# Norm sums that move the squares, in column quarters, and three smaller moves in a two-layer hybrid backbone

## Chip, cores and metric

The kernel runs on one core of a Trainium2 chip. The metric is the device time of one execution in microseconds; the time of a kernel is the median of its runs. TensorE is called PE in the profile, its weight loads PEld, VectorE DVE, ScalarE ACT, GpSimd POOL and SyncE SP; a q behind a name (SPq, ACTq) is that engine's queue of DMA issues and waits.

## The reference, cut to what matters

512 latent tokens and 256 context tokens of 1024 channels go through two layers. Layer 0 mixes by a Fourier transform beside a bidirectional state-space scan (SSD), layer 1 by differential attention of 8 heads beside a conformer convolution; each mixer and each feed-forward network (FFN) is framed by RMSNorms, and scaled and shifted by modulation vectors that come from the conditioning.

```python
def rmsnorm(x, g):
    xf = x.astype(jnp.float32)
    y = xf * lax.rsqrt(jnp.mean(xf * xf, axis=-1, keepdims=True) + NORM_EPS)
    return (y * g.astype(jnp.float32)).astype(x.dtype)
...
        m = (jax.nn.silu(c) @ mod_w[i] + mod_b[i]).reshape(-1, N_MOD, 1, D_MODEL)
        a_h = modulate(rmsnorm(h, g[0]), m[:, 0], m[:, 1])
        ...
        h = h + m[:, 2] * rmsnorm(o_h, g[1])
        f_h = swiglu(modulate(rmsnorm(h, g[2]), m[:, 3], m[:, 4]), ffn_w_gate[i], ffn_w_up[i], ffn_w_down[i])
        h = h + m[:, 5] * rmsnorm(f_h, g[3])
```

## The kernel before

Activations lie channel-major: 128 partitions by 8 channel groups (KT) by 768 tokens (T), the 512 latent tokens in front of the 256 of the context. Tokens are handled in three blocks of 256 (`BLK`, called a, b and c in the code; c is the context). Every large product runs in three passes over a split into a rounded part and its rest (`mm3`, L124; `split`, L97 on ScalarE and L98 on VectorE or GpSimd). Weights come in units of 512 KB through SyncE's queue into a few raw buffers (L108 for the mixers, L1189 for the FFNs), and a raw buffer is free for the next load when its split has read it. The program is traced in the written order; a scheduler with a cost model of the chip then sets the order on every engine. `tc.high_priority` and `tc.issue_after` push that order one way, and memory that a closed pool leaves is handed to the next one, whose first users wait for the last users of the old.

The stages, by the time of the profile: the first norm, the modulation vectors of layer 0 and the first projections (to about 130 us), the Fourier branch and the SSD groups (to 720), the end of the mixer and the FFN of layer 0 (to 1345), the attention with the conformer branch (to 1900), the FFN of layer 1 (to the end).

*Norms.* `rstd_stages` makes the reciprocal root for a block of 256 tokens. Squares come from ScalarE (`squares`, L290). PE then sums over channels: a group of 128 tokens of the squares is the stationary operand, one column of ones the moving one, 8 matmuls for each of 2 token groups (L263; f32 counts as two records each in the profile). The result has one column for each token group. ScalarE's root (L268) and a reciprocal on VectorE (L269) work on these two columns in the tile `nq`, and two matmuls with the reciprocals as stationary operand and the identity moving spread them over all partitions (L275). The `Turn` class strings these steps together with the residual additions: `r1` (squares and gates), `r2a`/`r2b` (norm of a branch's output and the addition), `q2`, `p1`, `p2` (norm of the sum, scale, shift and split into the inputs `xh`, `xl` of the next products), `last` for the end. Each 1024-channel norm of a block passes through `rstd_stages`; the norms of an attention head and of the conformer (one channel group, count 128 or 512) do too.

*Start.* `mod_sum` (L593) multiplies the two conditioning columns by raw modulation weights: two stationary columns, 512 moving ones, two matmuls for each of 8 groups, for vector 1 and then for vector 0. `mod_turn` copies the two rows out (L600) and turns them by eight narrow transposes (L603). Later vectors already use column quarters (`mod_quarters`, L196): four matmuls whose stationary operand is 32 wide, each writing another quarter of the partitions. The raw modulation weights pass through five buffers (L589).

*Between the mixer and the FFN of layer 0.* `turnc` handles the context block inside the SSD stage, in the pool `cp`; `h_c` is its residual, stored to the scratch `rd` (L1125). `res` then gets blocks a and b from the input and c from `rd` over ScalarE's queue (L1149, L1150). `pre0` turns a and b and stores all three blocks to `rd` (L1172). `hu` are the first three weight units of the FFN; `head(b)` runs them on a block as soon as it is ready.

*Attention.* For heads 0 to 6, four score blocks (`scores`, L1658 and L1662) each; between them `fills` are spread, first the next head's k, q and v, then what `extra` has for this head: `conv` (the conformer's convolution, L1544), `glu` (its gate, two weight units), `out_group` (output product of two finished heads). `conf_mean` and `conf_norm` follow a given head. Modulation vectors of layer 1 are summed on VectorE meanwhile (`mod_vec1`, L184 and L186), two weight loads for each score block of heads 0 to 3.

Of the kernel before, what the change touches and what calls it, by code (L numbers as in the profile page):

```python
# [21 lines left out]
KT = 8  # L22
# [34 lines left out]
def backbone_kernel(ctx, tc, xt, vec, dtrow, dskip, lam, w_mod, w_gate, w_up, w_down, w_in0, w_out0, w_in1, w_out1,  # L57
# [27 lines left out]
    qmask = cs[:, 640:644]  # L85
    eps = cst.tile([128, 1], F32, name="eps")
    nc.vector.memset(eps, EPS)
    newt = cst

    def vcol(off, n=1):  # L90
# [162 lines left out]
        return r  # L253

    fence = [None]

    def rstd_stages(psum1, sq, count, copy=True):
        n = sq.shape[-1]
        ps = psum1()
        kt = sq.shape[1]  # L260
        for h in range(n // 128):
            for k in range(kt):
                at = nc.tensor.matmul(ps[:, h:h + 1], sq[:, k, h * 128:h * 128 + 128], ones[:, 0:1], start=(k == 0),  # L263
                                      stop=(k == kt - 1))
        fence[0] = at.ins
        q = nrm[0].tile([128, 4], F32, tag="nq", name="nq", bufs=2)[:, 0:n // 128]
        if count == 1024:
            nc.scalar.activation(q, ps[:, 0:n // 128], AF.Sqrt, bias=eps, scale=1.0 / count)  # L268
            nc.vector.reciprocal(q, q)  # L269
        else:  # L270
            rsqrt(q, ps[:, 0:n // 128], count)
        yield None
        ps2 = psum1()
        for h in range(n // 128):
            at = nc.tensor.matmul(ps2[:, h * 128:h * 128 + 128], q[:, h:h + 1].to_broadcast([128, 128]), ident,  # L275
                                  start=True, stop=True)
        fence[0] = at.ins
        if not copy:
            yield ps2[:, 0:n]
            return  # L280
        r = nrm[0].tile([128, nrm[1]], F32, tag="nr", name="nr", bufs=512 // nrm[1])[:, 0:n]
        nc.scalar.copy(r, ps2[:, 0:n])
        yield r
# [233 lines left out]
    with ExitStack() as es:  # L517
# [71 lines left out]
            return raw, nc.sync.dma_start(out=raw, in_=w_mod[0, j, k]).ins  # L589

        def mod_sum(mps, raw, k):
            for n in range(2):
                nc.tensor.matmul(mps[n][0:2, :], silc[:, k, :], raw[:, n * 512:(n + 1) * 512],  # L593
                                 start=(k == 0), stop=(k == KT - 1))

        def mod_turn(mps, j):
            mrow = np_.tile([2, 1024], F32, tag="mrow", name="mrow", bufs=1)
            mt = psmm(2)[:, 0:16].rearrange("p (k w) -> p k w", w=2)
            for i in range(2):
                (nc.vector.tensor_copy, nc.scalar.copy)[i](mrow[:, i * 512:(i + 1) * 512], mps[i][0:2, :])  # L600
                for q in range(4):
                    b = i * 4 + q
                    turn = nc.tensor.transpose(mt[:, b, :], mrow[:, b * 128:(b + 1) * 128], ident[0:2, 0:2]).ins  # L603
            for w in range(2):
                nc.vector.tensor_tensor(out=mod[:, 0, w, j, :], in0=mt[:, :, w], in1=vcol(V_MODB + 8 * j, 8), op=ADD)
                mod_done(0, w, j)
            return turn

        mps = [psum1() for i in range(2)]
        load_x(BLK[0])  # L610
        nx = norm_x(BLK[0])
        for k in range(KT):
# [10 lines left out]
            load_x(b)  # L623
        hps = [psmm() for _ in hu]
        scaled(BLK[0])
        mps = [psum1() for i in range(2)]
        raws = [mod_raw(0, k)[0] for k in range(KT)]
        with tc.issue_after(turn):
            n1, n2 = (norm_x(b) for b in BLK[1:])
# [183 lines left out]
    with ExitStack() as es:  # L813
# [292 lines left out]
        for g in range(4):  # L1106
            if g < 3:
                xs = xbc_items(groups[g + 1])
                zs = sum([z_block(b) for b in zmap[g]], [])
                fills = merge(xs, zs)  # L1110
            else:
                state["acc"] = big.tile([128, KT, T], F32, tag="S0", name="acc")
                state["ys"] = big.tile([128, KT, T], F32R, tag="S1", name="ys")
                esx.close()
                cp = nrm[0] = pool(es, "cp", side="right")
                state["h"] = cp.tile([128, KT, 256], F32, name="h_c")
                nc.sync.dma_start(out=state["h"], in_=xt[:, :, BLK[2]])
# [27 lines left out]

    big2 = pool(ctx, "big2")
    res = big2.tile([128, KT, T], F32, tag="R", name="res")
    for b in BLK[:2]:
        nc.scalar.dma_start(out=res[:, :, b], in_=xt[:, :, b])  # L1149
    nc.scalar.dma_start(out=res[:, :, BLK[2]], in_=rd[:, :, BLK[2]])  # L1150
    xh = big2.tile([128, KT, T], F32R, tag="F0", name="xh")
    xl = big2.tile([128, KT, T], F32R, tag="F1", name="xl")

# [2 lines left out]
    def pre0(psum1, head):  # L1156
        c, a, b = BLK[2], BLK[0], BLK[1]
        t = turn0
        t.r1(a)
        t.p2(c)  # L1160
        t.r2(a, psum1)
        t.r1(b)
        head(c)
        t.q2(a)
        t.p1(a, psum1)
        t.r2(b, psum1)
        t.p2(a)
        t.q2(b)
        head(a)
        t.p2(b, psum1)  # L1170
        for blk in BLK:
            nc.scalar.dma_start(out=rd[:, :, blk], in_=res[:, :, blk])  # L1172
        head(b)
        return t.whole()
# [65 lines left out]
    def ffn(l, xh, xl, nt, pre, extra, post, spare):  # L1240
        with ExitStack() as es:
# [28 lines left out]
            todo = [(w, 2 * i + j) for i in range(NH // 2) for w in (0, 1) for j in range(2)]  # L1270
            if nu == 3:
                todo[1], todo[2] = todo[2], todo[1]
            hu = [wts.unit((w_gate, w_up)[w][l, i]) for w, i in todo[:nu]]
            hps = {wi: [bank() for _ in range(nt // 512 + (nt > 512))] for wi in todo[:nu]}

            def head(b):
# [152 lines left out]
    def post0(acc, psum1, accb):  # L1429
# [29 lines left out]
        t.p2(a)  # L1459
        fenced(c, range(3, KT))  # L1460
        t.r1(c)
        held, nrm[0] = nrm[0], cst
        t.r2a(c, psum1)
        nrm[0] = held
        t.q2(b)
        nc.scalar.dma_start(out=rd[:, :, b], in_=res[:, :, b])

# [5 lines left out]
    with ExitStack() as es:  # L1473
# [258 lines left out]
        def head1(b):  # L1732
            for u, p in list(zip(hu, hps))[3 if b.start == SEQ else 0:]:
# [21 lines left out]
        head_k(hs[0], hps[3])  # L1755
        head_v(hs[0], hps[4])

        extra = {0: [conv, lambda: glu(1)], 1: [conv, lambda: glu(2)], 2: [conv, lambda: glu(3)], 3: [conv],
                 4: [lambda: out_group((0, 1))], 5: [lambda: out_group((2, 3))]}
        late, later = [], []  # L1760
        macc = sxf[:, 4 * XN:4 * XN + 1024]

# [12 lines left out]
        for h in range(7):  # L1775
            H = hs[h]
            fills = [lambda: head_k(hs[h + 1]), lambda: head_q(hs[h + 1]), lambda: head_v(hs[h + 1])]
            fills += extra.get(h, [])
            n, done = len(fills), 0
            for qb in range(4):  # L1780
                p0 = scores(H, qb)
# [6 lines left out]
                if qb % 2 == 1:  # L1788
                    late.append(lambda H=H, qp=qb // 2: mix_v(H, qp))
                    if qb == 3:  # L1790
                        late.append(lambda H=H: sub_norm(H, LAT))
            if h == 4:
                csq = conf_mean()
            if h == 5:
                conf_norm(csq)


# [67 lines left out]
    turn2.h = Blocks({0: h_a, 256: res[:, :, b]})  # L1865

    def pre1(psum1, head):
        a, b = BLK[:2]
        turn2.r1(b)
        turn2.r2(b, psum1)  # L1870
# [142 lines left out]
```

## Time and profile before

| | |
|---|---|
| median of 3 runs | 2306.39 us (2297.15 to 2313.38) |
| the profiled execution | 2299.36 us, span 2297.6 us, mean granted clock 0.959 |
| PE busy | 2172.3 us, 95% of the span, 13742 matmul records |
| DVE, ACT, POOL busy | 1562.8, 1116.2, 758.9 us |
| read from and written to HBM | 206.51 MB and 19.63 MB |

The page gives the busy time of each engine, the chain of work that ended last, and groups of instructions by line. Other views used below: stretches (busy time of each engine between two times, with the clock that was granted to PE, the busy share of the DMA engines and GB/s; for one line alone if asked), the waits (who waited for whom, us in total, times, longest), the chain in order of time, and the instructions in order of time. A form such as "128x1 f32" is what a matmul moves, "128*32" the size of its stationary operand. Times are from the span's start.

### The profile page before, as it was taken

What the parts mean: (1) busy time and instruction counts of PE and PEld (TensorE: products, weight loads), DVE (VectorE), ACT (ScalarE), POOL (GpSimd) and SP (SyncE); (2) the same over time, 40 slices, a digit from 0 to 9 for tenths busy, and PEclk for the clock granted to TensorE, in tenths of its full rate; (3) what the DMA queues carried; (4) which work ended last, traced back from release to release, by engine and by line L of the source; (5) the groups of instructions that cost most, each with busy time, mean ns of one, the idle gap of its engine ahead of it and who ended that gap; (6) DMA issues with size and microseconds to landing.
All of it is one profiled execution on the core that took longest, in us unless ns stands there. A gap on an engine that the chain in (4) does not pass through costs nothing.

```text
span 2297.6 us, 35527 instructions
## 1 busy us (share of the span) xinstructions
PE 2172.3 (95%) x13742; PEld 1922.1 (84%) x13742; DVE 1562.8 (68%) x2551; ACT 1116.2 (49%) x2024; POOL 758.9 (33%) x703
## 2 busy tenths in 40 slices
PE   7999999898998999999999998999999888999998
PEld 3778888786787989999999997776777788999998
DVE  4722576677784566667767658767676855988985
ACT  4433586767452553333333444455555634644443
POOL 0201567676640023333334111011132110555550
PEclk9999999999999799999999979999999888999998
DMA  7344212223320533322122324555111221333321
GB/s 269 103 164 159 80 62 79 77 74 101 97 75 21 185 132 113 129 90 76 65 69 70 101 95 125 153 153 153 56 37 40 81 98 48 102 102 102 110 93 55
DMA packets 88776, 229.48 MB, mean 100 GB/s; under 512 B 8800, under 2 KB 39520, under 8 KB 88608
## 3 DMA queue, kind: packets, MB, share of 16 engines
q1 hardware_dynamic: 69584, 204.50, 27.0%
q10 hardware_dynamic: 17552, 17.61, 2.4%
q0 software_dynamic: 1472, 5.11, 0.6%
q8 instruction: 108, 1.77, 0.3%
q14 instruction: 60, 0.49, 0.1%
HBM read 206.51 MB, written 19.63 MB: 98 GB/s over the span
## 4 chain that ended last, share of the span: by engine, by line
PE 69%; DVE 13%; DMA 6%; ACT 6%; issue 3%; POOL 2%; ACTq 0%; SPq 0%; DVEq 0%; POOLq 0%
PE ps_mm L124 56%; DMA raw<-in_w_mod_dram 2%; PE ps_s L263 2%; DMA raw<-in_w_in_dram 2%; DVE w L98 1%; PE ps_s L196 1%; PE ps_s L593 1%; PE ps_mm L1544 1%; PE ps_s L911 1%; DMA mraw<-in_w_mod_dram 1%; DVE w L949 1%; PE ps_at L124 1%; ACT w L97 1%; DVE sx L186 1%; PE ps_S L1658 1%
## 5 line engine op out<-in xcount | busy, mean ns | idle before, releaser
L124 PE MATMUL ps_mm<-xh,w 128*128 128x256 f32 (+2 forms) x3600 | 844.3, 326 | 8.9 <-ACT xh L350 2.1
L124 PEld LDWEIGHTS ps_mm<-xh,w 128*128 128x128 f32 x3600 | 608.0, 194 | 62.6 <-issue 9.8
L124 PE MATMUL ps_mm<-xl,w 128*128 128x256 f32 (+2 forms) x1800 | 550.0, 323 | 5.5 <-POOL xl L324 2.6
L124 PE MATMUL ps_mm<-hid,w 128*128 128x384 f32 (+2 forms) x2244 | 391.9, 334 | 0.0
L124 PEld LDWEIGHTS ps_mm<-hid,w 128*128 128x128 f32 x2244 | 362.7, 192 | 20.9 <-issue 3.7
L98 DVE TENSOR_TENSOR w<-raw,w 128x512 fp32r<-128x512 f32 (+1 forms) x292 | 284.7, 982 | 109.9 <-ACT w L97 107.2
L124 PEld LDWEIGHTS ps_mm<-xl,w 128*128 128x128 f32 x1800 | 336.4, 194 | 26.3 <-DVE xl L351 3.0
L97 ACT CAST w<-raw 128x512 fp32r<-128x512 f32 (+1 forms) x323 | 239.2, 750 | 190.1 <-PE ps_mm L124 132.2
L98 POOL TENSOR_TENSOR w<-raw,w 128x1024 fp32r<-128x1024 f32 x31 | 76.7, 2474 | 329.8 <-ACT w L97 310.2
L1209 POOL TENSOR_TENSOR wt<-raw 128x512 f32<-128x512 f32 x78 | 117.9, 1512 | 202.0 <-DMA raw<-in_w_up_dram 134.5
L98 DVE TENSOR_TENSOR w<-wt,w 128x512 fp32r<-128x512 f32 x156 | 142.8, 925 | 58.0 <-ACT w L97 57.3
L97 ACT CAST w<-wt 128x512 fp32r<-128x512 f32 x156 | 93.9, 621 | 170.1 <-PE ps_mm L124 140.9
L1396 DVE TENSOR_TENSOR facc<-facc,ps_mm 128x384 f32<-128x384 f32 (+2 forms) x232 | 125.4, 564 | 73.1 <-PE ps_mm L124 72.5
L124 PE MATMUL ps_mm<-ys,w 128*128 128x256 f32 (+1 forms) x840 | 154.1, 337 | 12.3 <-DVE acc L493 4.4
L124 PEld LDWEIGHTS ps_mm<-ys,w 128*128 128x128 f32 x840 | 125.9, 196 | 32.3 <-DVE acc L493 7.8
L1209 POOL TENSOR_TENSOR wt<-raw,wt 128x512 f32<-128x512 f32 x39 | 59.4, 1522 | 216.1 <-DVE w L98 208.8
L124 PE MATMUL ps_mm<-w,xh 128*128 128x256 f32 x576 | 107.5, 287 | 0.7 <-ACT cin L867 0.7
L124 PEld LDWEIGHTS ps_mm<-w,xh 128*128 128x128 f32 x576 | 89.3, 189 | 5.5 <-ACT cin L867 1.3
L124 PE MATMUL ps_mm<-tq,w 128*128 128x384 f32 x480 | 89.8, 336 | 0.0
L124 PEld LDWEIGHTS ps_mm<-tq,w 128*128 128x128 f32 x480 | 83.8, 188 | 0.0
L124 PE MATMUL ps_mm<-w,xl 128*128 128x256 f32 x288 | 80.7, 280 | 0.0
L954 POOL TENSOR_TENSOR ex<-ex,w 128x384 f32<-128x384 f32 x48 | 59.5, 1241 | 58.7 <-ACT ex L953 49.8
(401 smaller groups left out, 3745.8 us busy)
## 6 DMA issues: line engine op xcount, KB each, us to landing
raw<-in_w_in_dram SPq DMA_DIRECT2D x69, 512.0 KB
mraw<-in_w_mod_dram SPq DMA_DIRECT2D x64, 512.0 KB
raw<-in_w_gate_dram SPq DMA_DIRECT2D x44, 512.0 KB
raw<-in_w_up_dram SPq DMA_DIRECT2D x44, 512.0 KB
raw<-in_w_down_dram SPq DMA_DIRECT2D x44, 512.0 KB
raw<-in_w_out_dram SPq DMA_DIRECT2D x32, 512.0 KB
raw<-in_w_mod_dram SPq DMA_DIRECT2D x32, 512.0 KB
res<-rd ACTq DMA_DIRECT2D x5, 1024.0 KB
```

The lines of the kernel that those rows point to most:

```text
L97: nc.scalar.copy(hi, raw)
L98: (eng or nc.vector).tensor_tensor(out=lo, in0=raw, in1=f32(hi), op=SUB)
L124: last = nc.tensor.matmul(dst, a, b[:, sl], start=(start and i == 0), stop=(stop and i == 2))
L186: nc.vector.scalar_tensor_tensor(out=acc, in0=raw, scalar=c, in1=acc, op0=MUL, op1=ADD)
L196: nc.tensor.matmul(ps[32 * q:32 * q + 32, 0:256], still, raw[:, q * 256:q * 256 + 256], start=start, stop=stop)
L263: at = nc.tensor.matmul(ps[:, h:h + 1], sq[:, k, h * 128:h * 128 + 128], ones[:, 0:1], start=(k == 0), stop=(k == kt - 1))
L593: nc.tensor.matmul(mps[n][0:2, :], silc[:, k, :], raw[:, n * 512:(n + 1) * 512], start=(k == 0), stop=(k == KT - 1))
L911: nc.tensor.matmul(ps[:, 0:GW], G.btok[:, c, :], xe, start=True, stop=True)
L949: nc.vector.scalar_tensor_tensor(out=w[:, h, :], in0=G.cb2[:, 1], scalar=dtt[:, c, r0 + 3 + h:r0 + 4 + h], in1=w[:, h, :], op0=MUL, op1=ADD)
L954: nc.gpsimd.tensor_tensor(out=ex, in0=ex, in1=w, op=MUL)
L1209: nc.gpsimd.tensor_tensor(out=t, in0=a, in1=b, op=op)
L1396: nc.vector.tensor_tensor(out=acc[:, m, s], in0=acc[:, m, s], in1=ps, op=ADD)
```

## The change

Five edits.

1. In `rstd_stages`, for more than one channel group: 32 columns of ones are the stationary operand and the squares move, a quarter of the block's tokens (64) to each quarter of the partitions, four matmuls for each channel group, channel group by channel group. `nq` becomes 128 by 64 values (32 equal rows in each quarter); the root takes 1024 times epsilon and leaves out the division, so that the spreading, four matmuls with a quarter's mask as stationary operand and `nq` moving, gives the reciprocal root as a sum of 32 equal rows. Norms of one channel group stay as they were, and their spreading no longer sets `fence`.
2. `nqp` says in which pool `nq` lies: `cst`, with one buffer, from the context's turn in the SSD stage until `pre0`, and from the end of `post0` until `pre1`; the stage's own pool with two buffers otherwise.
3. `mod_sum` and `mod_turn` use column quarters: one PSUM tile in place of two, four matmuls for a group with 256 moving columns, two wide transposes.
4. `res` gets only block a over ScalarE's queue; block b goes over SyncE's queue at the start of `pre0`, and block c is neither loaded nor stored there. The first of the FFN's early weight units is split into buffers of `modp` (layer 0).
5. In the attention, fills move: `conv` and `glu` from heads 0, 1, 2 and 3 to heads 0 to 4, the first `out_group` from head 4 to the front of head 5, the second from head 5 to head 6, `conf_mean` and `conf_norm` by one head.

```diff
+    eps32 = cst.tile([128, 1], F32, name="eps32")
+    nc.vector.memset(eps32, 1024 * EPS)
...
     def rstd_stages(psum1, sq, count, copy=True):
         n = sq.shape[-1]
         ps = psum1()
-        kt = sq.shape[1]
-        for h in range(n // 128):
-            for k in range(kt):
-                at = nc.tensor.matmul(ps[:, h:h + 1], sq[:, k, h * 128:h * 128 + 128], ones[:, 0:1], start=(k == 0),
-                                      stop=(k == kt - 1))
+        kt, w = sq.shape[1], n // 4
+        if kt == 1:
+            for h in range(n // 128):
+                at = nc.tensor.matmul(ps[:, h:h + 1], sq[:, 0, h * 128:h * 128 + 128], ones[:, 0:1], start=True,
+                                      stop=True)
+            w = n // 128
+
+        for k in range(kt if kt > 1 else 0):
+            for i in range(4):
+                at = nc.tensor.matmul(ps[32 * i:32 * i + 32, 0:w], ones[:, 0:32], sq[:, k, i * w:i * w + w],
+                                      start=(k == 0), stop=(k == kt - 1))
         fence[0] = at.ins
-        q = nrm[0].tile([128, 4], F32, tag="nq", name="nq", bufs=2)[:, 0:n // 128]
+        if kt == 1:
+            q = nrm[0].tile([128, 4], F32, tag="nq1", name="nq", bufs=2)[:, 0:w]
+        else:
+            q = (nqp[0] or nrm[0]).tile([128, 64], F32, tag="nq", name="nq", bufs=1 if nqp[0] else 2)
         if count == 1024:
-            nc.scalar.activation(q, ps[:, 0:n // 128], AF.Sqrt, bias=eps, scale=1.0 / count)
+            nc.scalar.activation(q, ps[:, 0:w], AF.Sqrt, bias=eps32, scale=1024.0 / count)
             nc.vector.reciprocal(q, q)
...
         ps2 = psum1()
-        for h in range(n // 128):
-            at = nc.tensor.matmul(ps2[:, h * 128:h * 128 + 128], q[:, h:h + 1].to_broadcast([128, 128]), ident,
-                                  start=True, stop=True)
-        fence[0] = at.ins
+        if kt == 1:
+            for h in range(w):
+                nc.tensor.matmul(ps2[:, h * 128:h * 128 + 128], q[:, h:h + 1].to_broadcast([128, 128]), ident,
+                                 start=True, stop=True)
+        else:
+            for i in range(4):
+                at = nc.tensor.matmul(ps2[:, i * w:i * w + w], qmask[:, i:i + 1].to_broadcast([128, 128]), q,
+                                      start=True, stop=True)
+            fence[0] = at.ins
...
         def mod_sum(mps, raw, k):
-            for n in range(2):
-                nc.tensor.matmul(mps[n][0:2, :], silc[:, k, :], raw[:, n * 512:(n + 1) * 512],
-                                 start=(k == 0), stop=(k == KT - 1))
+            for q in range(4):
+                nc.tensor.matmul(mps[32 * q:32 * q + 32, 0:256], silw[:, 2 * k:2 * k + 32],
+                                 raw[:, q * 256:q * 256 + 256], start=(k == 0), stop=(k == KT - 1))
...
-            mrow = np_.tile([2, 1024], F32, tag="mrow", name="mrow", bufs=1)
-            mt = psmm(2)[:, 0:16].rearrange("p (k w) -> p k w", w=2)
-            for i in range(2):
-                (nc.vector.tensor_copy, nc.scalar.copy)[i](mrow[:, i * 512:(i + 1) * 512], mps[i][0:2, :])
-                for q in range(4):
-                    b = i * 4 + q
-                    turn = nc.tensor.transpose(mt[:, b, :], mrow[:, b * 128:(b + 1) * 128], ident[0:2, 0:2]).ins
+            mrow = np_.tile([128, 256], F32, tag="mrow", name="mrow", bufs=1)
+            for h, e in enumerate((nc.vector.tensor_copy, nc.scalar.copy)):
+                e(mrow[:, h * 128:h * 128 + 128], mps[:, h * 128:h * 128 + 128])
+                turn = nc.tensor.transpose(mps[:, 256 + h * 128:384 + h * 128], mrow[:, h * 128:h * 128 + 128],
+                                           ident).ins
...
                 cp = nrm[0] = pool(es, "cp", side="right")
+                nqp[0] = cst
...
-    for b in BLK[:2]:
-        nc.scalar.dma_start(out=res[:, :, b], in_=xt[:, :, b])
-    nc.scalar.dma_start(out=res[:, :, BLK[2]], in_=rd[:, :, BLK[2]])
+    nc.scalar.dma_start(out=res[:, :, BLK[0]], in_=xt[:, :, BLK[0]])
...
     def pre0(psum1, head):
         c, a, b = BLK[2], BLK[0], BLK[1]
         t = turn0
+        nqp[0] = None
+        nc.sync.dma_start(out=res[:, :, b], in_=xt[:, :, b])
...
-        for blk in BLK:
+        for blk in BLK[:2]:
             nc.scalar.dma_start(out=rd[:, :, blk], in_=res[:, :, blk])
...
-            hu = [wts.unit((w_gate, w_up)[w][l, i]) for w, i in todo[:nu]]
+            hu = [wts.halves(wts.raw((w_gate, w_up)[w][l, i]), None if n else modp)
+                  for n, (w, i) in enumerate(todo[:nu])]
...
         t.r1(c)
-        held, nrm[0] = nrm[0], cst
+        nqp[0] = cst
         t.r2a(c, psum1)
-        nrm[0] = held
...
-        extra = {0: [conv, lambda: glu(1)], 1: [conv, lambda: glu(2)], 2: [conv, lambda: glu(3)], 3: [conv],
-                 4: [lambda: out_group((0, 1))], 5: [lambda: out_group((2, 3))]}
+        extra = {0: [conv, lambda: glu(1)], 1: [conv], 2: [lambda: glu(2)], 3: [conv, lambda: glu(3)], 4: [conv],
+                 6: [lambda: out_group((2, 3))]}
...
             fills += extra.get(h, [])
+            if h == 5:
+                fills.insert(0, lambda: out_group((0, 1)))
...
-            if h == 4:
+            if h == 5:
                 csq = conf_mean()
-            if h == 5:
+            if h == 6:
                 conf_norm(csq)
...
     def pre1(psum1, head):
+        nqp[0] = None
```

More of the change, by code (lines that the diff above doesn't have):

```diff
@@ L255, in backbone_kernel @@
     fence = [None]
+    nqp = [None]
     def rstd_stages(psum1, sq, count, copy=True):
@@ L259, in rstd_stages @@
         ps = psum1()
-        kt = sq.shape[1]
-        for h in range(n // 128):
-            for k in range(kt):
-                at = nc.tensor.matmul(ps[:, h:h + 1], sq[:, k, h * 128:h * 128 + 128], ones[:, 0:1], start=(k == 0),
-                                      stop=(k == kt - 1))
+        kt, w = sq.shape[1], n // 4
[8 more added lines that the diff above has]
+                                      start=(k == 0), stop=(k == kt - 1))
         fence[0] = at.ins
-        q = nrm[0].tile([128, 4], F32, tag="nq", name="nq", bufs=2)[:, 0:n // 128]
+        if kt == 1:
+            q = nrm[0].tile([128, 4], F32, tag="nq1", name="nq", bufs=2)[:, 0:w]
+        else:
+            q = (nqp[0] or nrm[0]).tile([128, 64], F32, tag="nq", name="nq", bufs=1 if nqp[0] else 2)
         if count == 1024:
-            nc.scalar.activation(q, ps[:, 0:n // 128], AF.Sqrt, bias=eps, scale=1.0 / count)
+            nc.scalar.activation(q, ps[:, 0:w], AF.Sqrt, bias=eps32, scale=1024.0 / count)
             nc.vector.reciprocal(q, q)
         else:
-            rsqrt(q, ps[:, 0:n // 128], count)
+            rsqrt(q, ps[:, 0:w], count)
         yield None
         ps2 = psum1()
-        for h in range(n // 128):
-            at = nc.tensor.matmul(ps2[:, h * 128:h * 128 + 128], q[:, h:h + 1].to_broadcast([128, 128]), ident,
-                                  start=True, stop=True)
-        fence[0] = at.ins
+        if kt == 1:
[7 more added lines that the diff above has]
+            fence[0] = at.ins
         if not copy:
@@ L591, in mod_sum @@
         def mod_sum(mps, raw, k):
-            for n in range(2):
-                nc.tensor.matmul(mps[n][0:2, :], silc[:, k, :], raw[:, n * 512:(n + 1) * 512],
-                                 start=(k == 0), stop=(k == KT - 1))
+            for q in range(4):
+                nc.tensor.matmul(mps[32 * q:32 * q + 32, 0:256], silw[:, 2 * k:2 * k + 32],
+                                 raw[:, q * 256:q * 256 + 256], start=(k == 0), stop=(k == KT - 1))
         def mod_turn(mps, j):
-            mrow = np_.tile([2, 1024], F32, tag="mrow", name="mrow", bufs=1)
-            mt = psmm(2)[:, 0:16].rearrange("p (k w) -> p k w", w=2)
-            for i in range(2):
-                (nc.vector.tensor_copy, nc.scalar.copy)[i](mrow[:, i * 512:(i + 1) * 512], mps[i][0:2, :])
-                for q in range(4):
-                    b = i * 4 + q
-                    turn = nc.tensor.transpose(mt[:, b, :], mrow[:, b * 128:(b + 1) * 128], ident[0:2, 0:2]).ins
+            mrow = np_.tile([128, 256], F32, tag="mrow", name="mrow", bufs=1)
[3 more added lines that the diff above has]
+                                           ident).ins
+            mt = mps[:, 256:512].rearrange("p (h q c) -> p q h c", h=2, q=4)
             for w in range(2):
-                nc.vector.tensor_tensor(out=mod[:, 0, w, j, :], in0=mt[:, :, w], in1=vcol(V_MODB + 8 * j, 8), op=ADD)
+                nc.vector.tensor_tensor(out=mod[:, 0, w, j, :].rearrange("p (q h) -> p q h", h=2), in0=mt[:, :, :, w],
+                                        in1=vcol(V_MODB + j * 8, 8).rearrange("p (q h) -> p q h", h=2), op=ADD)
                 mod_done(0, w, j)
             return turn
-        mps = [psum1() for i in range(2)]
+        mps = psum1()
         load_x(BLK[0])
@@ L625, in backbone_kernel @@
         scaled(BLK[0])
-        mps = [psum1() for i in range(2)]
+        mps = psum1()
         raws = [mod_raw(0, k)[0] for k in range(KT)]
```

## The prediction

> **What bounds the kernel now.** I read the page first, then the busy time of each engine by stretches, then the chain that ended last, and last the rows of the changed lines.
>
> ```profile
> span 2297.6 us, 35527 instructions
> PE 2172.3 (95%) x13742; PEld 1922.1 (84%) x13742; DVE 1562.8 (68%) x2551; ACT 1116.2 (49%) x2024; POOL 758.9 (33%) x703
> PE 69%; DVE 13%; DMA 6%; ACT 6%; issue 3%; POOL 2%; ACTq 0%; SPq 0%; DVEq 0%; POOLq 0%
> ```
>
> PE is busy 95% of the span and holds 69% of the chain, so what shortens PE's own work counts nearly in full wherever no other chain runs beside it. The stretches that the change touches (after the span: PE, PEld, DVE, ACT, POOL busy, then granted clock, DMA share, GB/s):
>
> ```profile
> 0.00:40.00 40.00, 23.38 (x70) 8.96 (x71) 15.01 (x27) 17.66 (x30) 3.31 (x5) 0.93 0.85 307
> 40.00:75.00 35.00, 35.00 (x201) 22.13 (x200) 22.05 (x38) 14.99 (x30) 5.11 (x2) 0.99 0.41 137
> 720.00:830.00 110.00, 100.96 (x687) 97.95 (x687) 69.02 (x129) 59.00 (x113) 5.76 (x4) 0.81 0.36 125
> 1295.00:1385.00 90.00, 88.41 (x657) 87.86 (x656) 48.42 (x99) 44.31 (x83) 7.18 (x3) 0.85 0.24 80
> 1840.00:1960.00 120.00, 104.04 (x719) 100.08 (x719) 72.51 (x134) 53.74 (x105) 7.89 (x6) 0.86 0.22 71
> 2255.00:2298.00 43.00, 31.80 (x251) 31.16 (x249) 18.29 (x36) 13.18 (x25) 0.00 (x0) 0.83 0.14 50
> ```
>
> The first row is the start, bound by transfers (0.85 of the DMA engines); the second is PE without a gap. The last four hold the residual turns with all 18 norms over 1024 channels: PE is busy 325.2 of 363 us there, at a granted clock of only 0.81 to 0.86.
>
> **1. The modulation sums of the start (L593).** First PE's time on that line in the two stretches, then its queue, the transfers, and the same sum in the quarter form, which other vectors use already (L196):
>
> ```profile
> 0.00:40.00 40.00, 16.64 (x32) 2.72 (x32) 0.93 0.85 307
> 40.00:75.00 35.00, 14.38 (x32) 2.39 (x32) 0.99 0.41 137
> SPq L589 <- PE ps_s L593: 14.8, 7, 3.7
> 12.00:14.00 2.00, 1.93 (x3) 0.37 (x4) 1.75 (x3) 1.97 (x4) 0.00 (x0) 1.00 1.04 416
> 16.00:18.00 2.00, 2.00 (x4) 0.21 (x2) 0.00 (x0) 0.00 (x0) 0.00 (x0) 1.00 0.57 156
> 33.81 0.23 DVE mod L605 x2
> 70.88 0.24 DVE mod L605 x2
> 203.45 1.86 PE ps_s L196 x32
> ```
>
> A quarter record costs 1.86/32 = 0.058 us. A vector goes from 32 records to 64, 3.7 us in place of 16.64 (first vector) and 14.38 (second). The vectors are written at 33.81 and 70.88 now. The first doesn't gain the whole difference of 13: SP's queue waited 14.8 us for L593 to give raw buffers back, and the transfers fell from 416 to 156 GB/s meanwhile. With the buffers free sooner the loads bound: 40 us at 307 GB/s are 12.3 MB, 29.5 us at 416, so at most 10.5 us sooner. I take 6, as the first load and the chain of small steps before the first projection stay. The second vector lies in a stretch where PE has no gap and DMA is at 0.41: 10.7 us less PE work, of which I take 7, because DVE (22.05 of 35) and ACT run chains between the blocks. The eight narrow transposes of each vector become two. The three norms of the start go from 8 sum records to 16 and stand at nothing: they run while PE waits for raw weights; without that cover, 24 x 0.058 = 1.4 us. **Term: -13 us** (bounds 0 and -21).
>
> **2. The norm sums.** PE on the sums (L263) and on the spreading matmuls (L275) in the last four stretches, together; then one norm at full clock, one at half; then the only matmuls of the kernel that move 64 columns of f32:
>
> ```profile
> sum 363.00, PE 85.04 PEld 86.11; mean PE 21.26 PEld 21.53
> sum 363.00, PE 16.57 PEld 13.90; mean PE 4.14 PEld 3.48
> 762.40 3.63 PE L263 MATMUL ps_s<-cs,sq 128*128 128x1 f32 x32
> 783.68 6.83 PE L263 MATMUL ps_s<-cs,sq 128*128 128x1 f32 x32
> L962 PE MATMUL ps_y<-xtok,ex 128*128 128x64 f32 x288 | 40.0, 274 | 6.8 <-POOL ex L954 6.6
> L695 DVE SCALAR_TENSOR_TENSOR p<-p,s x6: 446/457/460, 106.6 to 110.3; 128x288 f32<-128x288 f32 x6
> ```
>
> Now a norm loads 32 times 128 columns of squares to move one column each: 3.63 us, 0.113 a record. Afterwards it loads 32 columns of ones 64 times and moves 64 columns: 1152 records for 18 norms. The trace has no such record. From below: a quarter of L196's price, as a quarter of the columns moves, 0.0145 us, 17 us in all. From above: L962's 40.0/288 = 0.139, which holds whole 128-column loads, 160 us. Nearest is L196's 0.058, the same load with four times the columns, 67 us. I take 0.030, between the two quarter prices, since L196's four quarters run beside each other: 34.6 us, 50 less. Besides, an order by k lets all but the last pair of squares be summed while ScalarE still squares; now the second half of the tokens starts only when the first is through.
>
> The Trainium skill speaks against this: "TensorE: Matmul & The Clock Gate", section "Wait — 56ns, not 53.3ns?", has a floor of about 25 ns between starts, and of about 62 ns per matmul where the sequencer's microcode decodes. By estimate the 1152 records are 29 us by the first, 71 by the second. L196's 58 ns, with 256 columns streaming, is just under the second, so the trace agrees with the floor of 62 only loosely and excludes nothing below.
>
> The spreading goes from 4 records to 8 of the same load width, with 64 columns of the reciprocals moving: at most 16.57 more; the mask is there before the reciprocal is, so its first load is covered, and I take +11. ScalarE's root and the reciprocal run over 64 columns instead of 2: L695 works 288 columns in 0.457 us, so at most 0.1 us each for 62 more, +2 for 36 of them. Where nq lies in cst it has one buffer: the next root, and ScalarE's gates behind it, wait until it has been spread, 8 x 0.21 = 1.7 us after the one before; norms seldom follow so closely, so nothing. Net PE: -50 + 11 + 2 = -37. In the turns DVE's gate and add chains also end waits, so I let 60% of it through: **-22 us** (by the two ends (17 - 85) x 0.6 = -41 and (160 - 85 + 20) x 0.6 = +57).
>
> **3. The clock in these stretches.**
>
> ```profile
> 778.20:790.40 12.20, 10.11 (x49) 10.05 (x48) 6.64 (x17) 8.02 (x17) 0.01 (x1) 0.50 0.16 55
> 790.40:795.20 4.80, 4.80 (x23) 4.80 (x24) 0.86 (x5) 0.26 (x1) 0.00 (x0) 0.50 0.00 0
> 795.30:805.00 9.70, 9.70 (x87) 9.70 (x85) 5.06 (x7) 2.69 (x5) 0.00 (x0) 1.00 0.30 103
> ```
>
> From 783.68 on PE does little but L263, busy 10.11 of 12.2 us, and the clock stays at half; the projections behind it (790.4 on) run at 0.209 us a record and only after 795.3 at 0.111. So one-column records, busy as they look, don't bring the clock back. The four stretches lose 20.9 + 13.5 + 16.8 + 7.3 = 58.5 us of clock. Part of it is in the 85.04 already, part in real gaps; I take a tenth as recovered by shorter sums: **-6 us** (0 to -15).
>
> The same page, section "What's actually happening", says that a window of about 3.4 us of activity opens the clock; the rows above agree if one-column matmuls hardly count as activity. No run here shows whether 64 columns in four quarters count.
>
> **4. First weights and the context block's trips.**
>
> ```profile
> SPq L1189 <- DVE nq L269: 8.1, 2, 7.2
> ACT w L97 <- PE ps_mm L124: 2.7, 2, 2.3
> 755.69 0.34 SPq L1189 DMA_DIRECT2D raw<-in_w_gate_dram  x1
> 745.24 4.88 DMA rd<-h_c
> 750.14 10.00 DMA res<-rd
> 760.17 0.59 ACTq L1172 DMA_DIRECT2D rd<-res  x1
> 760.81 1.31 ACT L350 ACTIVATE xh<-acc,mod 128x256 fp32r<-128x256 f32 x3 [2.91 <-DVE xl L351]
> 765.89 0.36 PE L124 MATMUL ps_mm<-xh,w 128*128 128x256 f32 x1
> ```
>
> The first gate weights are issued at 755.69, because their buffer lies where the context norm's nq was (8.1 us waited). With nq in cst that wait goes; the first unit's halves move to modp and needn't wait for the last output weights (the casts waited 2.7 us for PE's reads of them). ACT's queue stood at the store of the context block (760.17), which waited for that block's load (10.00 us, itself behind the store of h_c), and the xh casts stood behind it (2.91 idle). Both go. Block b's load moves to SP, ahead of the later weights: 1 MB, 2.5 us at 416 GB/s, needed only in the second turn. But PE was summing until 766.03 and took up the projections at once, so weights alone give little until the sums before them are short; then they are what would be late. **-4 us** (0 to -10).
>
> **5. The later fill in the attention.** Heads 1, 2, 3, 4 and 6, from one score maximum to the next:
>
> ```profile
> 1456.40:1524.10 67.70, 63.74 (x389) 48.48 (x388) 45.97 (x76) 32.96 (x58) 9.35 (x7) 1.00 0.50 150
> 1524.10:1578.40 54.30, 51.48 (x317) 38.57 (x315) 38.60 (x70) 28.39 (x49) 6.24 (x4) 0.94 0.47 135
> 1578.40:1638.20 59.80, 56.23 (x332) 40.91 (x333) 40.49 (x70) 31.89 (x54) 9.11 (x5) 0.97 0.43 128
> 1638.20:1687.80 49.60, 44.62 (x245) 36.97 (x246) 35.06 (x61) 27.00 (x49) 8.99 (x5) 0.97 0.12 41
> 1740.80:1802.00 61.20, 52.83 (x276) 43.40 (x274) 43.54 (x83) 35.05 (x62) 15.49 (x9) 0.89 0.13 41
> SPq L108 <- DMA raw<-in_w_mod_dram: 45.6, 17, 6.0
> ```
>
> Work only moves: a glu and a convolution out of head 1, towards heads 3 and 4, output groups to heads 5 and 6. PE's gaps in heads 1, 3, 4 and 6 are 4.0, 3.6, 5.0 and 8.4 us; a perfect fill would close most of head 6's, and I give it 8 at most. Against it: head 3 gets a glu (two weight units more) while the queue of weights is still held up by the modulation loads (45.6 us of waiting), and the conformer norm now ends in head 6, right before head 7 needs its values. **0 us** (-8 to +10).
>
> **The sum:** -13 - 22 - 6 - 4 + 0 = -45. The profiled execution took 2299.36 us (span 2297.6), 7 below the median of 2306.39; 2254 for such an execution, and as a median 2258.
>
> **Rivals.**
> - *The records are bound by their number*, 0.058 us each. Sums 67, term 2 becomes (-18 + 13) x 0.6 = -3; the clock gives half, -3: 2299 - 13 - 3 - 3 - 4 = 2276, a median near 2280. For: no row of the trace is below 0.058. Against: there 256 columns stream. The skill's 62 ns would give this.
> - *The turns aren't PE's*: DVE chains end last and take term 2 down to -5. Then 2271. For: PE has 38 us of gaps there. Against: 790.40 to 805, without a gap on PE.
> - *The late conformer norm*: its reciprocal root, four multiplications and splits stand in front of head 7's first output product; term 5 is +10: 2264 to 2268.
> - *Slower*: the 32-column loads in quarters cost like whole ones, as at L962. At 0.139 us, term 2 is (75 + 13) x 0.6 = +53, term 3 zero: 2299 - 13 + 53 - 4 = 2335. It decides from about 0.087 us a record (1152 x 0.087 = 100; (15 + 13) x 0.6 = 17, what terms 1 and 4 bring). Against: L196's 0.058.
>
> **How the numbers follow.** Forecast 0.52, number-bound records 0.18, DVE's turns 0.12, late norm 0.10, slower 0.08. A measurement here tells about 1%, 23 us, from no change: below 2283 is faster. That holds for the forecast, mostly for the second and third rivals, half for the first. The order on every engine is laid out anew, and heads 1 and 2, with the same fill, already differ by 13 us (67.7 and 54.3), so some of each case falls above. Range 2230 to 2296: down to a full term 1 with 0.0145 us records, up past the first rival.
>
> **What would show it.** Right: no L593-like gap in the start, modulation j = 0 written before 60 us; sums of a norm below 2.2 us for 64 records at full clock; clock above 0.88 in the third stretch; first gate weights issued before 750. Wrong: a norm's 64 records above 3.6 us; PE idle in the turns rising by what the sums lost; a gap in head 7 before the first output product.

## The result, and the profile after

| | before | after |
|---|---|---|
| median of 4 runs | 2301.77 us (2295.73 to 2313.38) | 2246.31 us (2238.43 to 2252.29) |
| the profiled execution | 2299.36 us, span 2297.6 | 2252.29 us, span 2250.5 |
| mean granted clock | 0.959 | 0.973 |

The ratio is 0.9757 (95% interval 0.973 to 0.9784), faster. The forecast of 2258 us was 12 us too high, inside its range. The sum was made for the profiled execution, 2299 to 2254; that one stands at 2252, which is the slowest of its four runs. By the ratio the gain is 56 us, 11 more than the sum of 45; the two profiled executions are only 47 apart.

First the page of the changed kernel, from the span, the busy times and the chain that ended last; then its busy times by stretches (PE, PEld, DVE, ACT, POOL, then granted clock, DMA share, GB/s), for the same work as the six stretches of before:

```profile
span 2250.5 us, 36999 instructions
PE 2106.1 (94%) x14478; PEld 1855.2 (82%) x14478; DVE 1566.9 (70%) x2552; ACT 1115.4 (50%) x2024; POOL 756.8 (34%) x703
PE 70%; DVE 13%; ACT 6%; DMA 4%; issue 4%; POOL 2%; SPq 0%; ACTq 0%; DVEq 0%; POOLq 0%
...
0.00:30.00 30.00, 8.72 (x90) 3.31 (x90) 10.27 (x22) 13.63 (x23) 3.31 (x5) 0.87 0.92 331
30.00:62.00 32.00, 29.25 (x263) 25.16 (x264) 22.34 (x32) 15.45 (x28) 5.02 (x2) 0.85 0.64 223
700.00:810.00 110.00, 89.83 (x932) 82.54 (x931) 78.03 (x135) 61.88 (x116) 7.97 (x5) 0.86 0.31 106
1270.00:1360.00 90.00, 80.86 (x959) 77.12 (x959) 58.02 (x110) 47.29 (x88) 11.23 (x10) 0.98 0.33 108
1800.00:1920.00 120.00, 103.36 (x960) 96.16 (x959) 84.04 (x140) 58.01 (x108) 15.02 (x9) 0.91 0.32 102
2210.00:2251.00 41.00, 28.70 (x337) 26.89 (x335) 20.27 (x39) 13.43 (x25) 0.85 (x2) 0.88 0.15 52
```

PE does 736 records more in 66 us less, DVE and ACT the same as before. In the last four stretches PE now has gaps of 58 us in 361 (38 in 363 before), at a higher clock in each. By stages, each from one instruction to the same one in the other trace, before and after: the start to the SSD's inputs takes 166.1 to 155.0 us, the Fourier branch and the SSD 508.6 to 508.2, the turns until the FFN of layer 0 runs 235.1 to 225.7, the rest of that FFN **349.3 to 354.3**, the turn behind it up to the first score maximum 152.7 to 141.0, heads 0 to 6 390.2 to 379.3, the rest 495.6 to 487.1. Two of these weren't forecast: the heads' 10.9 us, and 5.0 us lost in a stage where nothing was edited.

### The profile page after: what moved, and what is told of

The parts are those of the page before. It is cut to its first block, busy times and chain, and to the rows that moved or that the text cites. A ratio compares the mean times of both kernels' runs of the same rounds, so it can differ in the third digit from the quotient of the medians.

```text
span 2250.5 us, 36999 instructions
## 1 busy us (share of the span) xinstructions
PE 2106.1 (94%) x14478; PEld 1855.2 (82%) x14478; DVE 1566.9 (70%) x2552; ACT 1115.4 (50%) x2024; POOL 756.8 (34%) x703
## 4 chain that ended last, share of the span: by engine, by line
PE 70%; DVE 13%; ACT 6%; DMA 4%; issue 4%; POOL 2%; SPq 0%; ACTq 0%; DVEq 0%; POOLq 0%
PE ps_mm L126 59%; DMA raw<-in_w_in_dram 2%; DMA raw<-in_w_mod_dram 2%; ACT w L99 1%; PE ps_s L198 1%; DVE w L100 1%; PE ps_mm L1562 1%; DVE sx L188 1%; PE ps_s L928 1%; PE ps_at L126 1%; DVE mx L1680 1%; DVE w L966 1%; PE ps_S L1676 1%; DMA mraw<-in_w_mod_dram 1%; PE ps_S L1672 1%
## 5 line engine op out<-in xcount | busy, mean ns | idle before, releaser
L126 PEld LDWEIGHTS ps_mm<-xh,w 128*128 128x128 f32 x3600 | 601.6, 192 | 80.6 <-issue 11.4
L1609 POOL TENSOR_TENSOR rs<-rs,rt 128x512 f32<-128x512 f32 x16 | 26.5, 1655 | 163.7 <-DVE rs L1608 143.9
```

Source lines behind the costliest of these rows:

```text
L126: last = nc.tensor.matmul(dst, a, b[:, sl], start=(start and i == 0), stop=(stop and i == 2))
L1609: nc.gpsimd.tensor_tensor(out=s, in0=s, in1=rt[:, 1], op=MUL)
```

## Experiments

Tile offset below is where the activation tiles (`ys`, `xh`, `xl`, and `hid`, the FFN's hidden values) start in a partition, modulo 128 bytes, by the addresses that the allocator gives them (some expectations count modulo 64). All begin at the same one, since they lie behind the constants pool, whose size the edits change. Each ratio is against runs of the kernel before that were made beside it (medians 2301.8 to 2303.6 us). Intervals are 95%.

| kernel | offset | median, us | ratio to before |
|---|---|---|---|
| `sums_only` | 0 | 2280.49 | 0.9898 (0.9874 to 0.9921) |
| `sums_pad` | 32 | 2276.82 | 0.9886 (0.9859 to 0.9913) |
| `mods_only` | 32 | 2297.45 | 0.9965 (0.9947 to 0.9983) |
| `loads_only` | 0 | 2311.37 | 1.0032 (1.0016 to 1.0048) |
| `loads_pad` | 32 | 2305.53 | 1.0021 (1.0001 to 1.004) |
| `fill_only` | 32 | 2295.99 | 0.9975 (0.9959 to 0.999) |
| `before_pad` | 64 | 2318.51 | 1.0081 (1.0051 to 1.0111) |
| the change | 0 | 2246.31 | 0.9757 (0.973 to 0.9784) |
| `after_pad` | 32 | 2237.66 | 0.9737 (0.9708 to 0.9766) |
| `no_loads_pad` | 32 | 2248.34 | 0.9769 (0.9747 to 0.9791) |
| `no_fill_pad` | 32 | 2250.76 | 0.9778 (0.9756 to 0.98) |
| `sums_x4` | 0 | 2298.53 | 0.9986 (0.9965 to 1.0006) |
| `quarters_in_turn` | 0 | 2283.06 | 0.9922 (0.9896 to 0.9948) |

**Each part alone.** The hunks of the diff for one part on the kernel before; `sums_only` is edit 1 and the pool of `nq` behind `post0`, `mods_only` edit 3, `loads_only` edits 2 and 4, `fill_only` edit 5.

> Only the norm sums and their spreading are in the new form (nq lies in cst from the end of layer 0's FFN to the start of layer 1's, without which it doesn't fit). Theory A, each edit acts in its own stage: the two traces are 24.5 us apart in the turns, of which the loads should hold some 4, so this is -20 us, ratio 0.991, with the start unchanged (the second modulation vector written near 71 us) and the half-clock time down from 190 to about 130 us. Rival B, the turns gain from the loads and the sums' records only free PE for DVE's chains: -8 us or less, ratio above 0.996. Rival C, a new order lets the attention shrink by itself: the heads 0 to 6 come out shorter than 390 us here too, without the fill moved.

> Only the two modulation sums of the start are in column quarters. Theory A: the start ends 10 to 12 us sooner and all else keeps its length: -11 us, ratio 0.995. Rival: the start ends as soon, but a later stage gives part back, as its loads then meet other transfers: -5 us.

> Only nq in cst, the first weight unit in modp, and the context block's load and store left out of res with block b on SP's queue. Theory A: -4 us (0 to -8), ratio 0.998, since PE is at the long norm sums when the weights come; the first gate weights are issued before 750 us. Rival: the queue of ACT was what held the turn, then -8 to -12.

> Only the attention's fills moved. Theory A, the fill made the 10.9 us by which heads 0 to 6 are shorter in the changed kernel: -11 us, ratio 0.995, heads 0 to 6 near 379 us. Rival, it is the laying out and the clock: within 4 us of the kernel before, heads 0 to 6 at 386 to 394 us.

By the ratios: sums -23 us, modulation sums -8, loads +7, fill -6, together -30, where the whole brought -56. The sums gave a little more than expected, though the half-clock time (the span times twice the missing share of the clock, 188 us before) fell only to 154 us and not to 130; the modulation sums came out between the theory and its rival; the loads issued their weights at 749.57, as said, but cost time instead of bringing 4; the fill brought half of its 11, with heads 0 to 6 at 378.5 us, as said. With the sums alone the heads took 394.4 us, so they don't shrink by themselves. So the parts help each other, or something is counted in two of them. In the trace of the loads alone, the FFN of layer 0 took 5 us more, as in the whole and with the sums alone, and with none of the others. Common to these three is the offset of the tiles.

**The place of the tiles.** One unused column in the constants pool moves everything behind it by 32 bytes:

```diff
+    pad = cst.tile([128, 1], F32, name="pad")
+    nc.vector.memset(pad, 0.0)
     newt = cst
```

> The changed kernel with one unused column (32 B) more in the constants pool, so that every activation tile behind it starts at 32 modulo 64 bytes, as before the change, and not at 0. Theory A (where a moving operand starts sets the spacing of its records): 128x384 records at 173.3 ns and not 175.6, 128x512 of hid at 228.9 and not 233.3; the 1949 records of layer 0's Strassen stretch take 349.3 us and not 354.3; in all 8 to 12 us less, a median of 2234 to 2238. Theory B (the spacing comes from the order or from what runs beside it): spacing as in the changed kernel, 2246 within 4.

> The kernel before with the same unused column: its activation tiles move from 32 to 0 modulo 64 bytes, and nothing else changes. Theory A: 128x384 records at 175.6 ns, 128x512 of hid at 233.3, 8 to 12 us slower, a ratio of 1.0035 to 1.005. Theory B: 173.3 and 228.9 ns, a ratio of 1.000 within 0.0015.

> The sooner first weights and the changed trips of the residual alone (which were 0.3% slower than before), with the unused column, so that the tiles stand at 32 modulo 64 as before. Theory A: the loss of 7 to 11 us was the place of the tiles; now a ratio of 0.997 to 1.000, the forecast's 0 to 10 us for this edit. Theory B: the loads themselves cost it, ratio 1.003 again.

The stretch of the FFN of layer 0 (an expectation calls it the Strassen stretch) between two fixed instructions of POOL, in which PE never stops, as busy time of PE alone (records, clock, DMA share, GB/s), for before, before padded, after, after padded:

```profile
909.81:1259.08 349.27, 349.27 (x2067) 1.00 0.25 82
...
917.11:1272.68 355.57, 355.57 (x2068) 1.00 0.23 81
...
888.77:1243.12 354.35, 354.35 (x2067) 1.00 0.26 81
...
887.42:1236.69 349.27, 349.27 (x2068) 1.00 0.26 82
```

The same records (1949 of the projections, the rest modulation sums) at full clock take 349.27 us at offset 32, 354.35 at 0 and 355.57 at 64. By the starts of successive records in the trace, those that move 128x384 of `hid` come every 173.3 ns at offset 32, 175.6 at 0 and 176.6 at 64. Theory A holds in both directions. No edit acts on it but through the offset: from the same start to the next semaphore event of POOL, the stretch takes 349.4 us in all eight kernels at offset 32, 354.5 to 354.6 in all five at 0 and 355.7 in the one at 64. The pad in the kernel before cost more than expected, 16.7 us, of which 6.3 lie in this stretch; it went to 64 and not to 0, and at 64 the 256-column records are slower too (119.2 ns against 117.8 for `xh`). The padded change is the fastest kernel that ran, 2237.66 us; its interval overlaps that of the change, but the 5 us of this stretch are beyond doubt. For the loads, only a part of the loss was the place: 1.0032 became 1.0021, where 1.000 or less was expected.

**What a sum costs, and who sets the turns.** `sums_x4` does each sum matmul four times:

```diff
-            for i in range(4):
-                at = nc.tensor.matmul(...)
+            for rep in range(4):
+                for i in range(4):
+                    at = nc.tensor.matmul(...)
```

> The changed kernel with every sum matmul of the norms done four times (the root's scale takes out the factor): 4608 records in place of 1152 in the four turn stretches, some 86 us more on PE at the 0.025 us a record that the changed kernel shows. If the turns are bound by PE (the forecast's 60% and more comes through): 45 to 80 us slower than the changed kernel, 2290 to 2325. If DVE's and ScalarE's chains set them: up to 25 us slower, below 2271, and PE's idle time there falls by the rest. If 64-column quarters count as activity for the clock, the half-clock time falls from 122 us although PE does nothing new.

`quarters_in_turn` exchanges the two loops:

```diff
-        for k in range(kt if kt > 1 else 0):
-            for i in range(4):
+        for i in range(4 if kt > 1 else 0):
+            for k in range(kt):
```

> The changed kernel with the sum matmuls ordered quarter by quarter (eight records of one quarter in a row) and not channel group by channel group, so that no two quarters run beside each other. If the 0.017 to 0.025 us a record come from quarters that overlap: about 0.054 us a record (64 columns streaming alone), 33 us more on PE, 20 to 40 us slower than the changed kernel, 2266 to 2286. If the price is a matter of the load's width and of issue alone: 2246 within 6, as the later start of the sums costs little.

PE's time on the sums in the four stretches for the change, `sums_x4` and `quarters_in_turn`; then one norm's 64 records at full clock in the change and in `quarters_in_turn`; last, all engines in the four stretches of `sums_x4`:

```profile
sum 361.00, PE 28.79 PEld 20.91; mean PE 7.20 PEld 5.23
...
sum 414.00, PE 80.33 PEld 73.38; mean PE 20.08 PEld 18.35
...
sum 411.00, PE 71.01 PEld 61.91; mean PE 17.75 PEld 15.48
...
747.26 1.10 PE L272 MATMUL ps_s<-sq,cs 128*32 128x64 f32 x64
...
748.11 3.18 PE L272 MATMUL ps_s<-sq,cs 128*32 128x64 f32 x64
...
sum 414.00, PE 359.04 PEld 342.11 DVE 248.74 ACT 192.33 POOL 38.17; mean PE 89.76 PEld 85.53 DVE 62.19 ACT 48.08 POOL 9.54
```

Four times the records took 80.33 us, 0.017 each, not the 115 expected: that is the price of the 64 records above at full clock (1.10 us), while the change's mean of 0.025 has short series and half clock in it. It is 51.5 us more on PE, and the kernel was 52.2 us slower than the change; PE's gaps in the four stretches stay (55 us, 58 in the change). So all of what is added to the sums reaches the end. A sum is also a link of its norm's own chain, between the squares and the root, so this run doesn't tell whether PE's queue or that chain lets it through. The half-clock time of the whole, 116 us for 122, is too near to tell anything; a burst shown at the end does.

In turn, a quarter at a time, 1152 records cost 71.01 us, 0.062 each, 42.2 us more, and the time rose by 36.8, within what was expected. By the starts of the records at full clock, those of one quarter come every 56 ns in both orders. In the change the records of the other three quarters start in between, 7 ns apart, so that four take the time of one. The low price is this overlap, and not a cheaper record.

**The sums, at the old place.**

> Norm sums in quarters alone, activation tiles at 32 modulo 64 bytes as before the change. Sums alone with the tiles at 0 stood at 23 us less. If the place of the tiles was a loss of its own on top (8.6 us in the whole change), 29 to 35 us less than before, ratio 0.985 to 0.987: about the forecast's terms 2 and 3 together (-28). If the place matters only in the whole, 0.990 again.

-26.1 us, between the 23 and the 29 to 35 that were expected. PE alone from the end of the SSD to the FFN of layer 0, and from there to the first score maximum, before and with the sums:

```profile
674.80:909.80 235.00, 220.75 (x1411) 0.91 0.31 110
1259.10:1411.80 152.70, 146.13 (x1015) 0.89 0.34 107
...
679.50:908.20 228.70, 205.45 (x1628) 0.93 0.33 113
1257.50:1395.50 138.00, 126.10 (x1226) 0.96 0.37 115
1395.50:1793.20 397.70, 364.44 (x2111) 0.96 0.32 97
```

Of 35.3 us that PE no longer works in the first two stretches, 21.0 come out as time and 14.3 as new gaps. The last row is heads 0 to 6: 397.7 us against 390.2, so 7.5 us go again there. By stages this trace gains 6.3 and 14.7 us in the two stretches and 12.4 behind the heads, 33.4 in all, and loses the 7.5 in the heads and 4.8 before the SSD's inputs (170.9 us against 166.1). Why it loses there is open; `sums_only` loses 1.9 at the start and 4.2 in the heads.

**Parts left out of the whole.** Both at offset 32, against `after_pad`: without edits 2 and 4 before the FFN of layer 0, and without edit 5.

> The whole change without the sooner first weights (residual trips as before, first weight units in the old buffers, the norm's values of the context turn in that turn's pool), tiles at 32 modulo 64. If these edits cost what they cost alone (0.2 to 0.3%), 4 to 8 us faster than the padded whole at 2237.7: 2230 to 2234. If they are worth the forecast's 4 us once the sums are short: 2240 to 2246.

> The whole change without the later fill, tiles at 32 modulo 64. If the fill is worth in the whole what it was alone (0.25%): 2241 to 2247. If it is also what keeps the heads from losing 4 us, as they did with the sums alone and with the loads alone: 2249 to 2256. If it is worth nothing, as forecast: 2238.

The loads that cost 0.2% alone are worth 0.3% here, against the first expectation and more than the second: 2248.34 for 2237.66. The intervals of the two ratios overlap, but each of the four runs (2246.8 and more) is longer than any of `after_pad` (up to 2244.2). In the chain that ended last, `no_loads_pad` has first the trip of the context block, the store that waits for it at the head of ACT's queue, and the projections behind; `after_pad` starts them 9.1 us sooner (the last row):

```profile
739.02 14.99 DMA res<-rd
...
754.03 0.59 ACTq L1191
...
757.33 5.74 PE ps_mm L128 x29
...
748.24 4.86 PE ps_mm L128 x26
```

In the kernel before, the chain passes through this trip as well (it landed at 760.14, as the prediction shows), but PE was summing until 766.03 in any case. From the end of the SSD to the FFN, the loads bring 0.6 us with the old sums (235.1 to 234.5 in `loads_pad`) and 9.3 with the new ones (234.3 to 225.0).

PE alone in heads 0 to 6, and from there to the end, for before, `fill_only`, `no_fill_pad` and `after_pad`:

```profile
1411.80:1802.00 390.20, 363.12 (x2106) 0.97 0.32 97
1802.00:2297.60 495.60, 464.52 (x3242) 0.94 0.27 89
...
1410.60:1789.10 378.50, 360.88 (x2077) 0.97 0.30 98
1789.10:2291.60 502.50, 469.73 (x3271) 0.94 0.26 90
...
1373.90:1772.60 398.70, 367.60 (x2111) 0.95 0.32 96
1772.60:2248.80 476.20, 440.19 (x3458) 0.96 0.29 93
...
1374.30:1752.60 378.30, 359.75 (x2082) 0.98 0.32 99
1752.60:2242.40 489.80, 454.37 (x3487) 0.95 0.29 92
```

The later fill closes gaps: 27.1 us of them in the heads become 17.6, and 31.1 become 18.5 in the whole. 29 records move past head 6, and part of what the heads save (11.7 and 20.4 us) is given back behind them (6.9 and 13.6). Net it is 6 us alone and, by the ratios, 9 in the whole, as expected if the fill is also what keeps the heads short.

## Why the prediction was right, step by step

**Term 1, the start (-13): right in sum, its halves wrong.** -11.1 us at the SSD's inputs, -8.1 by the ratio of `mods_only`. The new sums take more than forecast (3.7 us each; the rows below say 6.53 and 5.29), since they come in bursts of 8 records as the loads land, most of 0.64 us and some of 1.08, and mostly not in one series. The chain that ended last, with the two vectors and the load between them:

```profile
0.00:30.00 30.00, 6.53 (x64) 1.42 (x64) 0.87 0.92 331
30.00:62.00 32.00, 5.29 (x64) 2.04 (x64) 0.85 0.64 223
...
25.35 0.23 DVE mod L621 x2
...
40.95 3.94 DMA mraw<-in_w_mod_dram
...
61.23 0.24 DVE mod L621 x2
```

The first vector comes 8.5 us sooner (6 forecast), the second 9.65 (13 forecast): it adds 1.2 and not 7, and it is written at 61.23 where the sign of being right said before 60. What is late next is the raw weights (3.94 us of waiting for a load in the chain), and the clock: PE now has gaps there (29.25 of 32 us busy, 35 of 35 before), and 0.85 is granted where it was 0.99.

**Term 2, the norm sums (-22), and term 3, the clock (-6): right together, -26.1 with the tiles in place, in part by luck.** The record was 0.025 us in the turns, 0.017 in a series at full clock, not 0.030: sums -56.3 us of PE, not -50. One norm takes 1.10 us at full clock; 2.2 was set as the sign. The spreading was over-sized and the reciprocal under-sized (the first row is PE on the spreading in the four stretches, against 16.57 before):

```profile
sum 361.00, PE 20.49 PEld 19.21; mean PE 5.12 PEld 4.80
...
L281 DVE RECIPROCAL nq<-nq x21: 539/553/556, 15.5 to 2239.6; 128x64 f32<-128x64 f32 x21
...
L269 DVE RECIPROCAL nq<-nq x21: 154/165/167, 19.4 to 2287.5; 128x2 f32<-128x2 f32 x21
```

+4 us and not +11; +0.39 us for each reciprocal, where L695's multiplications had given 0.1 at most: a reciprocal isn't priced by them. With these sizes the prediction's own formula gives (-56.3 + 3.9 + 18 x 0.39) x 0.6 = -27, and -33 with the 6 for the clock. That is what the stretches with the turns gave in the trace of `sums_pad`, 33.4; the losses at the start, where the prediction put the norms at nothing, and in the heads bring the whole back to the forecast's size. The 60% let through is what the turns of layer 0 show, 21.0 of 35.3 us. It isn't a constant: work added there counts in full (`sums_x4`), work removed until other chains show: PE's gaps in the four stretches rose by 20 us where the sums lost 56, so that the sign of being wrong that names them came in part. The half-clock time fell from 188 to 122 us in the two traces (138 in that of `after_pad`), the stretches stand at 0.86, 0.98, 0.91 and 0.88 (above 0.88 in the third of these four, as said); how much of this is a term of its own can't be told from the sums' shorter time.

The Trainium skill ("TensorE: Matmul & The Clock Gate", section "Wait — 56ns, not 53.3ns?") gave two floors, 25 and 62 ns. The second is out: 32 matmuls, 64 records, take 1.10 us. By records, (1.10 - 0.22)/63 = 14 ns lie between starts on average (0.22 is the record's own length), below the first floor too; by matmuls, 28 ns, just above it. (The prediction counted both by records; by matmuls its estimates are 14 and 36 us.) The mean per matmul agrees with 25, but the single starts don't: neighbouring quarters start 7 ns apart. What sets the mean here is the 56 ns within a quarter, shared by four. In L196's 256-column records the same distance is 216 ns, so the prediction's lower price, a quarter of L196's (0.0145 us), is the one that holds in a series at full clock. The record's length is the median of this row (ns):

```profile
L272 PE MATMUL ps_s<-sq,cs x576: 218/219/318, 714.7 to 2238.7; 128*32 128x64 f32 x192
```

**Term 4, first weights and trips (-4): the sentence was right, the size low.** First gate weights are issued at 735.50 (before 750, as said, though `no_loads_pad`, without the edit, issues them at 742.70, so that this sign didn't test it), and the wait for the reciprocal fell from 8.1 to 1.2 us:

```profile
735.50 1.38 SPq L1207 DMA_DIRECT2D raw<-in_w_gate_dram  x1
...
SPq L1207 <- DVE nq L281: 1.2, 1, 1.2
```

"Weights alone give little until the sums before them are short; then they are what would be late" is what the runs show: +4.8 us alone (1.0021), -7.4 in the whole (0.9769 to 0.9737), -9.3 in their stage.

**Term 5, the later fill (0): mis-sized.** The 8 us "at most" were the gap of head 6; the gaps of all heads together shrank by 9.5. What was set against it hardly came. The sums on VectorE wait less for modulation weights in the heads (before, after: us, times, longest), and PE's gaps in head 7 grew by 2.8 us, from 1.8 to 4.6, which is all that could be left of the late conformer norm:

```profile
DVE sx L186 <- DMA raw<-in_w_mod_dram: 19.4, 14, 4.8
...
DVE sx L188 <- DMA raw<-in_w_mod_dram: 11.8, 9, 2.7
...
1802.00:1834.10 32.10, 30.27 (x188) 0.87 0.29 103
...
1763.40:1790.90 27.50, 22.88 (x121) 0.94 0.13 39
```

**The rivals.** *Number-bound records* (0.058 us, 2280) fell with 0.025; `quarters_in_turn`, where quarters don't overlap, shows that world: 0.062 us a record, 2283. *DVE's turns* left 11 us for terms 2 and 3 together, and fell with the 26.1 of `sums_pad`. *The late norm* is at most 2.8 of its 10 us. *Slower* needed 0.087 us a record.

**What it left out** is the place of the tiles, 8.6 us against the change by the medians (2246.31 and 2237.66; 4.6 by the ratios), and that the parts need each other. By the ratios and with the tiles at 32, the parts alone make -26.2 (sums), -8.1, +4.8 and -5.8, or -35; the padded whole is -60. The loads explain 12 of the missing 25, the fill 4. The rest, some 9 us, stays open. By the intervals of the ratios the 25 is good to some 12 us, the 12 to 10 and the 4 to 9, so the fill's part and the rest may be nothing. Open is also why the heads take 398 us in `sums_pad`, `loads_pad` and `no_fill_pad`, 8 more than before. A single trace can't settle a few us: runs of the kernel before lie between 2288 and 2313.

The forecast's median has a slip too: with the profiled execution 7 us below the median, 2254 gives 2261 and not 2258, 15 us above what was measured.

## What to carry to other kernels

Price a matmul by what it moves and by whether neighbours can run beside it: a reduction with ones as the narrow stationary operand, with neighbouring matmuls in different column quarters, cost a third of the same reduction with the data stationary here, and its order of loops alone was worth 37 us. An edit that gains nothing alone may be the next limit: test it in the whole, by leaving it out, before dropping it. And when a stage that wasn't edited changes its pace, look at where the allocator put its tiles.

## What the hardware showed that was not expected

- The start of the tiles, 32, 0 or 64 modulo 128 bytes, sets PE's pace at full clock: 349.27, 354.35 and 355.57 us for the same stretch. An offset of 96 wasn't tried, and neither was which operand or engine makes it.
- Records of 64 columns follow each other every 56 ns within one column quarter, whether the other three quarters work in between or not; those of four quarters start 7 ns apart.
- 64-column quarter records count as activity for the clock, which the prediction left open. In `sums_x4` one burst of 256 sum records, with nothing else on PE, begins at half clock and goes on at full:

```profile
777.42 6.14 PE L275 MATMUL ps_s<-sq,cs 128*32 128x64 f32 x256
...
777.45:781.50 4.05, 4.05 (x157) 0.50 0.02 4
781.60:783.50 1.90, 1.78 (x109) 1.00 0.00 0
```

  After some 4 us of sums the full clock is back; the one-column records of before ran for 6.83 us from 783.68 and left it at half until 795. The Trainium skill's window of about 3.4 us ("TensorE: Matmul & The Clock Gate", section "What's actually happening") agrees with the burst.
- VectorE's reciprocal takes 0.553 us for 64 columns and 0.165 for 2, 6.3 ns a column; the multiplications of L695 run at 1.6.
